# Bias vectors in 23 shifted copies instead of 128, and tables read from them in longer runs

## The chip, the cores and the metric

The kernel runs on one core of a Trainium2 chip. The metric is the device time of one launch in microseconds (us): the median of a few runs. One further execution was taken with the hardware profiler, and all rows below come from it. The engines are TensorE (PE, matmuls; PEld is its weight load), VectorE (DVE), ScalarE (ACT), GpSimd (POOL) and SyncE (SP, which issues the DMAs here).

## What is computed

The reference is two networks, one after the other, over 256 tokens of width 1024: a block of feed-forward, retention and differential attention in two layers, and a second block in two layers, of feed-forward, a mixer, and feed-forward. The mixer of the second block's first layer is a short convolution, that of its second layer a dilated attention with three groups. Only that attention uses the data that the change touches: a learned bias by distance, the same along each diagonal of a score matrix.

```python
def band_bias(rel_bias_g, dilation, n_steps):
    i = jnp.arange(BLOCK)[:, None]
    j = jnp.arange(2 * BLOCK)[None, :]
    step = BLOCK + i - j
    in_band = (step >= 0) & (step <= n_steps)
    bucket = t5_bucket(jnp.clip(step, 0, n_steps) * dilation)
    bias = rel_bias_g[bucket]
    return jnp.transpose(bias, (2, 0, 1)).astype(jnp.float32), in_band
...
    logits = jnp.einsum('bsnqhd,bsnkhd->bsnhqk', qs, kb) + bias
```

All matmuls of weights are done in three parts (high by high, high by low, low by high) to keep single precision.

## The kernel before

**Weights.** All weights pass once, in order, through a stream of units. A unit is a tile of 128 partitions by up to 2048 numbers (1 MB). `issue_dma` (line 113) has SP load it into `raw`, of which there are four buffers; `pre_act` (L127) makes the high part `whi` on ACT, in two halves, and `pre_dve` (L136) the low part `wlo` on DVE. When the second half's low part is written, the unit's `raw` buffer is free and SP may load the unit four places on. `whi` and `wlo` have three buffers. SP works through its DMAs strictly in the order of the program, and all of them go out on one queue.

**Feed-forward.** `ffn` takes 22 units of gate and up weights (`gu...`), each of them 48 matmuls of 128x256 at L161, and then 16 units of the down product (`dn...`), whose eight results are added into `h` at L291. Near its start, `norm_end` (L249) reads the sum of squares of the layer before.

**Bias vectors.** `bias_vectors` is called just ahead of the second block's first-layer second feed-forward. For each of five tables `v` it makes a vector of 256 numbers for each of 16 heads: a matmul with a one-hot matrix (L801) and a copy to `bt` (L802), a tile on 16 partitions, one for each head. Then five DMAs (L804), put into the program by `later` four slots apart, write `bt` to the DRAM tensor `ztab`: each vector 128 times, one copy for each partition of the later tables.

**Tables.** The attention of the last layer works on four heads at a time, from nine weight units (three groups of queries, keys and values; L920). `load_table` (L818) reads a head's table from `ztab` to a tile `tab` of 128 partitions by 5 by 128 numbers. A row pitch of 255 within copies of 256 shifts each partition by one number against the last, which gives the diagonals. `scores` adds the table to the products of queries and keys in one DVE instruction (L858), which also gives the row's extreme value; ACT takes the exponential. For queries and keys, ACT squares the product into `qsq` (L933), and DVE sums it (L935). `out1` writes `aon` on DVE (L886), which PE then transposes.

Which instruction of an engine comes where is settled when the program is built, by a scheduler that works with estimated durations; every engine then runs its own list in order.

Of the kernel before, what the change touches and what calls it, by code (L numbers as in the profile page):

```python
# [29 lines left out]
NG = 144  # L30

C_ID, C_RC, C_RS, C_DC, C_DS, C_MASK, C_DEC = 0, 128, 400, 672, 944, 1216, 1488
NC1 = 1488 + 4 * 272
# [5 lines left out]
def build(ctx, tc, ins, out, upto=None):  # L39
# [3 lines left out]

    # ------------------------------------------------------------------ pools
    keep = ctx.enter_context(tc.tile_pool(name="keep", bufs=1))
# [34 lines left out]
    qk_g = keep.tile([128, 6], F32, name="qk_g")  # L80
    ztab = dram.tile([16, 5, 128, 256], F32, name="ztab")

    # --------------------------------------------------------- weight stream
    units = []
# [32 lines left out]
    def pre_act(most=2):  # L117
        """High parts of the next half units, as far as the slots reach."""
        while most and st["half"] // 2 < min(st["done"] + NSPLIT, NU):
            i, b = divmod(st["half"], 2)  # L120
            n = units[i][1] // 2
            if b == 0:
                his[i] = (wp.tile([128, 2048], F32R, tag="whi", name="whi"),
                          wp.tile([128, 2048], F32R, tag="wlo", name="wlo"))
            hi, lo = his[i]
            c = slice(b * n, b * n + n)
            ACT.activation(hi[:, c], raws[i][:, c], AF.Copy)  # L127
            pend.append((i, b, c))
            st["half"] += 1
            most -= 1  # L130

    def pre_dve():
        """Low parts of what pre_act has done."""
        for i, b, c in pend:
            hi, lo = his[i]
            DVE.tensor_tensor(out=lo[:, c], in0=raws[i][:, c], in1=hi[:, c], op=ALU.subtract)  # L136
            if b == 1:
                raws.pop(i)
                issue_dma(i + 1 + NRAW)
        pend.clear()  # L140
# [15 lines left out]

    # ------------------------------------------------------- small utilities
    def mm3(ps, wh, wl, xh, xl, start, stop, late=False):
# [37 lines left out]

    # ------------------------------------------------------------------ norms
    # The gain goes into the split operand; the factor of a token goes into
    # the results of the products that use it.
    nst = {}  # L200
# [37 lines left out]
    def norm_end():  # L238
        T = nst["T"]
        ms = bank("o")  # L240
        PE.matmul(ms[:, 0:T], ones, nst["ssq"][:, 0:T], start=True, stop=True)
        if nst["fin"] is not None:
            ms2 = bank("t")
            PE.matmul(ms2[:, 0:T], ones, nst["ssq2"][:, 0:T], start=True, stop=True)
        x = nrm.tile([128, T1], F32, tag="nx", name="nx", bufs=1)
        t = nrm.tile([128, T1], F32, tag="nt", name="nt", bufs=1)
        r = nrm.tile([128, T1], F32, tag="r", name="r")
        xv, tv, rv = x[:, 0:T], t[:, 0:T], r[:, 0:T]
        DVE.tensor_scalar(out=xv, in0=ms[:, 0:T], scalar1=EPS, scalar2=None, op0=ALU.add)  # L249
        fin = nst["fin"]  # L250
        if fin is None:
            rsqrt_wide(xv, rv, tv)
            return r
        # Both norms in one factor: 1 / ((ms + eps) (ms2 / (ms + eps) + eps)).
        x2 = nrm.tile([128, T1], F32, tag="nx2", name="nx2", bufs=1)
        DVE.scalar_tensor_tensor(out=x2[:, 0:T], in0=xv, scalar=EPS, in1=ms2[:, 0:T], op0=ALU.mult, op1=ALU.add)
        rsqrt_wide(x2[:, 0:T], rv, tv)

        def residual():
            r1 = nrm.tile([128, T1], F32, tag="r", name="r1")  # L260
            t1 = nrm.tile([128, T1], F32, tag="nx2", name="t1", bufs=1)
            rsqrt_wide(xv, r1[:, 0:T], t1[:, 0:T])
            for d in range(KD):
                hv = h[:, d, T1 - T:T1]
                DVE.scalar_tensor_tensor(out=hv, in0=hv, scalar=fin[:, d:d + 1], in1=r1[:, 0:T],
                                         op0=ALU.mult, op1=ALU.mult)
        later(8, residual)
        return r
# [15 lines left out]

    # ------------------------------------------------------- products into h
    def add_to_h(d, ps, scale, T, perm=False):
# [6 lines left out]
    def out_product(yhi, ylo, order, off, T, first, nxt, perm=False, ready=None):  # L293
        """[1024 x 1024] product into h; its first `first` outputs wait with
        their last two K tiles for what is still under way."""
        tiles = {}
# [112 lines left out]

    # ------------------------------------------- retention + diff attention  # L410
    swap_pair = [i ^ 1 for i in range(32)]
    swap_half = [(i ^ 8) if i < 16 else i for i in range(32)]

    def mix_first(l, cst, nxt):
# [27 lines left out]

        # values: to token-major
        d_cols = ((0, 16), (16, 144), (144, 272))
# [14 lines left out]

        # differential attention of one head  # L460
        dsmall = {}
# [91 lines left out]

        # the first 16 queries of all differential heads
        def small_scores():
# [65 lines left out]

        # retention of one head: token tiles (0, 128), (128, 256), (256, 272)
        def ret_scores(hd):
# [115 lines left out]

    # -------------------------------------------------------------- conv mixer  # L740
    def mix_conv(nxt):
# [48 lines left out]

    # ------------------------------------------------------- dilated attention
    def bias_vectors(sb):
        hot = sb.tile([33, 5, 256], F32, name="hot")
        rb = sb.tile([33, 48], F32, name="rb")
        bt = sb.tile([16, 5, 256], F32, name="bt")
        SP.dma_start(hot, ins["onehot"].rearrange("b (v x) -> b v x", v=5))
        POOL.memset(rb[32:33, :], NEG)
        SP.dma_start(rb[0:32, :], ins["rel_bias"])
        for v, g in enumerate((0, 1, 2, 0, 0)):
            p = bank("t", 16, (256,))  # L800
            PE.matmul(p, rb[:, g * 16:(g + 1) * 16], hot[:, v, :], start=True, stop=True)  # L801
            ACT.activation(bt[:, v, :], p, AF.Copy)  # L802
        for v in range(5):
            later(4 * v, lambda v=v: SP.dma_start(ztab[:, v, :, :], bt[:, v:v + 1, :].to_broadcast([16, 128, 256])))  # L804

    def mix_attn(nxt):
# [7 lines left out]
        def load_table(hd):  # L814
            t = tmp.tile([128, 5, 128], F32, tag="tab", name="tab", bufs=4)
            z = ztab[hd]
            src = bass.AP(tensor=z.tensor, offset=z.offset + 127, ap=[[255, 128], [128 * 256, 5], [1, 128]])
            SP.dma_start(t, src)  # L818
            tabs[hd] = t.rearrange("p v x -> p (v x)")

        def turn(qd, g, w, ps, f):
            """Normalised queries or keys of four heads to feature-major."""
            qn = tmp.tile([128, 8, 64], F32, tag="qn", name="qn")
# [14 lines left out]
        def scores(qd, pr, a):  # L838
            """Two heads, in the two row halves of the array."""
            if flight["n"] >= 2:  # L840
# [3 lines left out]
            s = [bank("b") for i in range(2)]  # L844
            # column, group, first key, keys
            blocks = (((0, 1, 0, 128), (128, 2, 0, 128), (256, 0, 0, 256)) if a == 0 else
# [6 lines left out]
            for i in range(2):  # L853
                hq = pr * 2 + i
                tab = tabs[qd["i"] * 4 + hq][:, 128 - 128 * a:640 - 128 * a]
                e = tmp.tile([128, 512], F32, tag="e", name="e", bufs=3)
                nm = tmp.tile([128, 1], F32, tag="anm", name="anm", bufs=3)
                DVE.tensor_tensor_reduce(out=e, in0=s[i], in1=tab, scale=-1.0, scalar=3e38, op0=ALU.add, op1=ALU.min,  # L858
                                         accum_out=nm)
# [23 lines left out]
        def out1(qd):  # L883
            DVE.reciprocal(qd["sum"], qd["sum"])
            on = tmp.tile([128, 8, 64], F32, tag="aon", name="aon")
            DVE.tensor_tensor(out=on, in0=qd["o"].rearrange("p a h d -> p (a h) d"),  # L886
# [16 lines left out]
        for qi in range(4):  # L903
# [5 lines left out]
            for g in range(3):  # L909
                for w in range(3):  # L910
# [19 lines left out]
                    else:  # L930
                        sq = tmp.tile([128, 8, 64], F32, tag="qsq", name="qsq")
                        ss, x, y, t = (tmp.tile([128, 2, 4], F32, tag="q" + n, name="q" + n, bufs=3) for n in "sxyt")
# [23 lines left out]

    # ---------------------------------------------------------------- program
    def gcol(c):
# [109 lines left out]

# [1 line left out]
def _tiles(w):  # L1070
    """[K, M] -> [M / 128, 128, K / 128, 128]: for each 128 columns, the rows by partition."""
    K, M = w.shape
# [119 lines left out]
```

## Time and profile before

| | us |
|---|---|
| median of 3 runs | 2331.13 (2330.07 to 2332.43) |
| span of the profiled execution | 2330.6 |
| PE busy | 2249.6 (97%) |
| DVE busy | 1567.0 (67%) |
| ACT busy | 1063.3 (46%) |
| POOL busy | 165.6 (7%) |

The profiled execution's time is its span, 2330.6 us, so it lies within the three runs. The profile gives for each engine the busy time, the busy share in 40 slices of the span, the clock that TensorE was granted, the bytes that the DMA engines moved, and a chain: the work that ended last, followed back from the last instruction to what released each step. A PE that is busy for 97% of the span leaves few places where another engine or a DMA can be what ends last; the slices show where these are.

### The profile page before, as it was taken

What the parts mean: (1) busy time and instruction counts of PE and PEld (TensorE: products, weight loads), DVE (VectorE), ACT (ScalarE), POOL (GpSimd) and SP (SyncE); (2) the same over time, 40 slices, a digit from 0 to 9 for tenths busy, and PEclk for the clock granted to TensorE, in tenths of its full rate; (3) what the DMA queues carried; (4) which work ended last, traced back from release to release, by engine and by line L of the source; (5) the groups of instructions that cost most, each with busy time, mean ns of one, the idle gap of its engine ahead of it and who ended that gap; (6) DMA issues with size and microseconds to landing.
All of it is one profiled execution on the core that took longest, in us unless ns stands there. A gap on an engine that the chain in (4) does not pass through costs nothing.

```text
span 2330.6 us, 43868 instructions
## 1 busy us (share of the span) xinstructions
PE 2249.6 (97%) x18324; PEld 2211.8 (95%) x18324; DVE 1567.0 (67%) x2880; ACT 1063.3 (46%) x1721; POOL 165.6 (7%) x590
## 2 busy tenths in 40 slices
PE   9999999999999999999999995499999999999999
PEld 9999989999999998999999995499999999999999
DVE  7766878766765877766975873375875555545874
ACT  5444435444444444545444441244444455555543
POOL 1000140000000021000000000000000333330000
PEclk9999999999999999999999997699999999999999
DMA  7546325445545433546545568845545644442543
GB/s 278 175 140 211 127 91 182 175 149 201 181 141 194 154 127 132 192 151 214 183 164 198 199 172 137 207 158 202 196 170 176 220 156 168 141 164 94 186 154 130
DMA packets 80514, 395.58 MB, mean 170 GB/s; under 512 B 7067, under 2 KB 28827, under 8 KB 46012
## 3 DMA queue, kind: packets, MB, share of 16 engines
q1 hardware_dynamic: 80316, 392.78, 50.5%
q8 instruction: 143, 2.34, 0.4%
q14 instruction: 55, 0.45, 0.1%
HBM read 381.22 MB, written 11.53 MB: 169 GB/s over the span
## 4 chain that ended last, share of the span: by engine, by line
PE 90%; DMA 4%; DVE 2%; POOL 1%; issue 1%; ACT 1%; SPq 0%; POOLq 0%; ACTq 0%; DVEq 0%
PE ps_mm L161 42%; PE ps_b L161 23%; PE ps_a L161 11%; PE ps_mm L920 9%; DMA raw<-in_gu2b_dram 4%; PE ps_o L877 1%; PE ps_b L851 1%; DVE wlo L136 1%; PE ps_a L866 1%; POOL rt L192 1%; PE ps_t L832 0%; PE ps_b L469 0%; ACT whi L127 0%; DMA h<-in_h_dram 0%; POOL ry L195 0%
## 5 line engine op out<-in xcount | busy, mean ns | idle before, releaser
L136 DVE TENSOR_TENSOR wlo<-raw,whi 128x1024 fp32r<-128x1024 f32 (+1 forms) x792 | 857.7, 1114 | 332.0 <-ACT whi L127 331.4
L127 ACT ACTIVATE whi<-raw 128x1024 fp32r<-128x1024 f32 (+1 forms) x792 | 730.5, 966 | 737.1 <-issue 311.5
L161 PE MATMUL ps_mm<-xhi,wlo 128*128 128x256 f32 (+1 forms) x1904 | 544.0, 286 | 0.5 <-DVE wlo L136 0.5
L161 PE MATMUL ps_mm<-xlo,whi 128*128 128x256 f32 (+1 forms) x1904 | 541.9, 285 | 0.0
L161 PE MATMUL ps_mm<-xhi,whi 128*128 128x256 f32 (+1 forms) x1904 | 534.8, 286 | 0.0
L161 PEld LDWEIGHTS ps_mm<-xhi,wlo 128*128 128x128 f32 x1904 | 359.5, 189 | 3.2 <-issue 2.2
L161 PEld LDWEIGHTS ps_mm<-xlo,whi 128*128 128x128 f32 x1904 | 358.9, 189 | 2.1 <-issue 1.9
L161 PEld LDWEIGHTS ps_mm<-xhi,whi 128*128 128x128 f32 x1904 | 359.2, 189 | 1.4 <-issue 1.1
L161 PE MATMUL ps_b<-xhi,wlo 128*128 128x256 f32 (+1 forms) x1032 | 296.5, 288 | 50.4 <-DVE wlo L136 49.7
L161 PE MATMUL ps_b<-xlo,whi 128*128 128x256 f32 (+1 forms) x1032 | 295.4, 286 | 0.0
L161 PE MATMUL ps_b<-xhi,whi 128*128 128x256 f32 (+1 forms) x1032 | 290.9, 287 | 0.0
L161 PEld LDWEIGHTS ps_b<-xhi,wlo 128*128 128x128 f32 x1032 | 197.0, 191 | 52.3 <-DVE wlo L136 50.3
L161 PE MATMUL ps_mm<-fh,wlo 128*128 128x256 f32 (+1 forms) x704 | 199.4, 283 | 0.0
L161 PE MATMUL ps_mm<-fh,whi 128*128 128x256 f32 (+1 forms) x704 | 199.0, 283 | 0.0
L161 PE MATMUL ps_mm<-fl,whi 128*128 128x256 f32 (+1 forms) x704 | 198.9, 283 | 0.0
L161 PEld LDWEIGHTS ps_b<-xlo,whi 128*128 128x128 f32 x1032 | 196.9, 191 | 0.6 <-issue 0.4
L161 PEld LDWEIGHTS ps_b<-xhi,whi 128*128 128x128 f32 x1032 | 197.1, 191 | 0.1
L373 ACT ACTIVATE th<-gs 128x256 f32<-128x256 f32 (+1 forms) x176 | 72.7, 420 | 262.4 <-DVE gs L372 262.4
L920 PE MATMUL ps_mm<-wlo,xhi 128*128 128x256 f32 x576 | 164.2, 286 | 1.9 <-ACT vT L929 1.9
L920 PE MATMUL ps_mm<-whi,xlo 128*128 128x256 f32 x576 | 164.2, 285 | 0.0
L920 PE MATMUL ps_mm<-whi,xhi 128*128 128x256 f32 x576 | 163.0, 283 | 0.0
L161 PE MATMUL ps_a<-xhi,wlo 128*128 128x256 f32 (+1 forms) x520 | 148.9, 286 | 12.1 <-DVE wlo L136 10.9
(353 smaller groups left out, 4322.0 us busy)
## 6 DMA issues: line engine op xcount, KB each, us to landing
raw<-in_gu_dram SPq DMA_DIRECT2D x87, 1024.0 KB, 4.8
raw<-in_dn_dram SPq DMA_DIRECT2D x64, 704.0 KB, 4.1
raw<-in_gu1b_dram SPq DMA_DIRECT2D x44, 1024.0 KB, 4.8
raw<-in_gu2b_dram SPq DMA_DIRECT2D x44, 1024.0 KB, 4.8
raw<-in_qkv_dram SPq DMA_DIRECT2D x36, 1024.0 KB, 4.8
raw<-in_win_dram SPq DMA_DIRECT2D x28, 1024.0 KB, 4.8
raw<-in_dn1b_dram SPq DMA_DIRECT2D x32, 704.0 KB, 4.1
raw<-in_dn2b_dram SPq DMA_DIRECT2D x32, 704.0 KB, 4.0
```

Source lines behind the costliest of these rows:

```text
L127: ACT.activation(hi[:, c], raws[i][:, c], AF.Copy)
L136: DVE.tensor_tensor(out=lo[:, c], in0=raws[i][:, c], in1=hi[:, c], op=ALU.subtract)
L161: PE.matmul(ps, a, b, start=start and i == 0, stop=stop and i == 2)
L192: POOL.tensor_tensor(out=t, in0=y, in1=y, op=ALU.mult)
L373: ACT.activation(th[:, 0:T], gs[:, 0:T], AF.Tanh, scale=0.5)
L851: PE.matmul(s[i][:, c:c + n], q[p, pr, g, a * 128:a * 128 + 128], k[p, pr, g, k0:k0 + n], start=True, stop=True)
L866: PE.transpose(tp[:, b, :], e[:, b * 128:(b + 1) * 128], ident)
L877: PE.matmul(qd["o"][:, a, hq, :], pT[:, b, :], qd["v"][:, kt, g, hq * 64:hq * 64 + 64], start=b == 0, stop=b == 3)
L920: PE.matmul(ps[:, a, :], x, y, start=k == 0 and n == 0, stop=k == KD - 1 and n == 2)
```

## The change

The bias vectors of a head are kept together, as one run of 5 x 256 = 1280 numbers, and this run is stored 23 times for each head, by four DMAs of 6, 6, 6 and 5 copies. Each of them now needs all of `bt`. Partition p = 8a + b of a table takes copy a + b, from the place 127 - p on, so that 16 + 8 - 1 = 23 copies are enough. `load_table` reads 1152 numbers in one run for each partition, where there were five runs of 128. Of these 1152 each of the two score blocks uses four pieces of 128, 256 apart, so the DVE instruction of `scores` now has operands of 4 by 128. `tab` grows from 640 to 1152 numbers a partition, in four buffers; `qsq` and `aon` go from two buffers to one. The diff also removes comments, which shifts line numbers.

```diff
+NCOPY = 15 + 7 + 1
...
-    ztab = dram.tile([16, 5, 128, 256], F32, name="ztab")
+    ztab = dram.tile([16, NCOPY, 1280], F32, name="ztab")
...
-        for v in range(5):
-            later(4 * v, lambda v=v: SP.dma_start(ztab[:, v, :, :], bt[:, v:v + 1, :].to_broadcast([16, 128, 256])))
+        for c in range(0, NCOPY, 6):
+            n = min(6, NCOPY - c)
+            later(2 * c, lambda c=c, n=n: SP.dma_start(
+                ztab[:, c:c + n, :], bt.rearrange("h v x -> h (v x)").unsqueeze(1).to_broadcast([16, n, 1280])))
...
-            t = tmp.tile([128, 5, 128], F32, tag="tab", name="tab", bufs=4)
+            t = tmp.tile([128, 1152], F32, tag="tab", name="tab", bufs=4)
             z = ztab[hd]
-            src = bass.AP(tensor=z.tensor, offset=z.offset + 127, ap=[[255, 128], [128 * 256, 5], [1, 128]])
+            src = bass.AP(tensor=z.tensor, offset=z.offset + 127, ap=[[1280 - 8, 16], [1280 - 1, 8], [1, 1152]])
             SP.dma_start(t, src)
-            tabs[hd] = t.rearrange("p v x -> p (v x)")
+            tabs[hd] = (t[:, 128:1152].rearrange("p (v x) -> p v x", v=4)[:, :, 128:256],
+                        t[:, 0:1024].rearrange("p (v x) -> p v x", v=4)[:, :, 0:128])
...
-                tab = tabs[qd["i"] * 4 + hq][:, 128 - 128 * a:640 - 128 * a]
+                tab = tabs[qd["i"] * 4 + hq][a]
...
-                DVE.tensor_tensor_reduce(out=e, in0=s[i], in1=tab, scale=-1.0, scalar=3e38, op0=ALU.add, op1=ALU.min,
+                ev, sv = (z.rearrange("p (v x) -> p v x", v=4) for z in (e, s[i]))
+                DVE.tensor_tensor_reduce(out=ev, in0=sv, in1=tab, scale=-1.0, scalar=3e38, op0=ALU.add, op1=ALU.min,
                                          accum_out=nm)
...
-            on = tmp.tile([128, 8, 64], F32, tag="aon", name="aon")
+            on = tmp.tile([128, 8, 64], F32, tag="aon", name="aon", bufs=1)
...
-                        sq = tmp.tile([128, 8, 64], F32, tag="qsq", name="qsq")
+                        sq = tmp.tile([128, 8, 64], F32, tag="qsq", name="qsq", bufs=1)
```

The program's order changes in two places, and by a few rows on each engine. On SP, in the feed-forward that follows `bias_vectors`, the list before reads as follows (`hot` and `rb` are the one-hot matrix and the biases, `raw<-in_gu2b_dram` is a weight unit):

```order
L796 DMA hot<-in_onehot_dram 33x1280
L798 DMA rb<-in_rel_bias_dram 32x48
L113 DMA raw<-in_gu2b_dram 128x2048
L804 DMA ztab<-bt 16x128x256 x2
L113 DMA raw<-in_gu2b_dram 128x2048
L804 DMA ztab<-bt 16x128x256
L113 DMA raw<-in_gu2b_dram 128x2048
L804 DMA ztab<-bt 16x128x256 x2
L113 DMA raw<-in_gu2b_dram 128x2048 x13
```

And after the change:

```order
L798 DMA hot<-in_onehot_dram 33x1280
L800 DMA rb<-in_rel_bias_dram 32x48
L115 DMA raw<-in_gu2b_dram 128x2048 x3
L807 DMA ztab<-bt 16x6x1280 x3
L807 DMA ztab<-bt 16x5x1280
L115 DMA raw<-in_gu2b_dram 128x2048 x13
```

Two weight units that stood behind two and three stores now stand ahead of all of them, and the four stores follow one another.

On ACT, at the first queries and keys of the attention (`qsq` the squares, `whi` high parts of weights, `vT` the values), before:

```order
L127 ACTIVATE whi<-raw 128x1024
L933 ACTIVATE qsq<-ps_mm 128x512
L127 ACTIVATE whi<-raw 128x1024 x2
L933 ACTIVATE qsq<-ps_mm 128x512
L127 ACTIVATE whi<-raw 128x1024 x2
L929 ACTIVATE vT<-ps_mm,rc 128x256 x2
```

And after the change:

```order
L129 ACTIVATE whi<-raw 128x1024
L939 ACTIVATE qsq<-ps_mm 128x512
L129 ACTIVATE whi<-raw 128x1024 x3
L939 ACTIVATE qsq<-ps_mm 128x512
L129 ACTIVATE whi<-raw 128x1024
L935 ACTIVATE vT<-ps_mm,rc 128x256 x2
```

One high part moved from behind the second square to ahead of it.

## Rows read from the trace of the kernel before

**Rows 1.** The page: span, and busy tenths of PE in 40 slices.

```profile
span 2330.6 us, 43868 instructions
...
PE   9999999999999999999999995499999999999999
```

**Rows 2.** Chain of work, 1350 to 1560 us: start us, us, what (xcount).

```profile
1386.37 0.53 PE ps_t L801 x2
...
1391.04 59.40 DMA raw<-in_gu2b_dram x2
...
1454.12 37.74 DMA raw<-in_gu2b_dram
...
1494.31 5.49 PE ps_b L161 x24
...
1505.87 2.84 PE ps_mm L161 x24
```

**Rows 3.** Stretches of two feed-forwards: length, then PE, PEld, DVE, ACT, POOL busy; PEclk.

```profile
1384.88:1633.41 248.53, 189.75 (x1534) 186.70 (x1533) 129.86 (x215) 87.27 (x136) 0.00 (x0) 0.88 0.69 174
1640.77:1821.22 180.45, 180.45 (x1527) 180.28 (x1526) 130.25 (x215) 85.94 (x132) 0.00 (x0) 1.00 0.53 182
```

**Rows 4.** PE by line, 1384.88 to 1633.41: busy, mean ns | idle before, releaser.

```profile
L161 PE MATMUL ps_b<-xhi,wlo 128*128 128x256 f32 x113 | 33.9, 300 | 47.9 <-DVE wlo L136 47.2 <-issue 0.7
...
L161 PE MATMUL ps_a<-xhi,wlo 128*128 128x256 f32 x52 | 15.6, 300 | 10.9 <-DVE wlo L136 10.9
...
L801 PE MATMUL ps_t<-hot,rb 33*16 33x256 f32 x8 | 2.4, 382 | 0.0
```

**Rows 5.** DMA issues of the whole span: xcount, KB each, median us to landing.

```profile
raw<-in_gu2b_dram SPq DMA_DIRECT2D x44, 1024.0 KB, 4.8
...
ztab<-bt SPq DMA_DIRECT2D x5, 2048.0 KB, 38.3
...
tab<-ztab SPq DMA_DIRECT2D x16, 320.0 KB, 5.2
```

**Rows 6.** DMA, 1395 to 1400 us, where only `ztab` stores run.

```profile
DMA packets 503, 0.52 MB, mean 103 GB/s; under 512 B 0, under 2 KB 503, under 8 KB 503
```

**Rows 7.** DMA, 2328.4 to 2328.9 us: the last store of `h` from 128 partitions.

```profile
DMA packets 142, 0.13 MB, mean 262 GB/s; under 512 B 14, under 2 KB 142, under 8 KB 142
```

**Rows 8.** SP in order of time, 1376 to 1500 us: start us, us.

```profile
1383.60 7.34 SPq L804 DMA_DIRECT2D ztab<-bt  x2
1391.04 19.42 SPq L113 DMA_DIRECT2D raw<-in_gu2b_dram  x1
```

**Rows 9.** ACT in order of time, 1380 to 1500 us [idle before <-releaser].

```profile
1398.95 0.35 ACT L802 ACTIVATE bt<-ps_t 16x256 f32<-16x256 f32 x1
...
1429.88 2.00 ACT L127 ACTIVATE whi<-raw 128x1024 fp32r<-128x1024 f32 x2 [21.51 <-DMA raw<-in_gu2b_dram]
```

**Rows 10.** PE alone, 1421 to 1422 us: length, busy (xcount), PEclk, DMA share, GB/s.

```profile
1421.00:1422.00 1.00, 0.34 (x3) 1.00 0.82 101
```

**Rows 11.** DMA, 1824.9 to 1830.4 us, while the first four tables land.

```profile
DMA packets 2695, 1.77 MB, mean 322 GB/s; under 512 B 80, under 2 KB 2640, under 8 KB 2640
```

**Rows 12.** Stretches of the attention: columns as Rows 3, then DMA share, GB/s.

```profile
1821.00:1870.00 49.00, 47.13 (x387) 46.93 (x386) 27.49 (x42) 23.08 (x31) 21.68 (x70) 0.97 0.59 200
1870.00:1920.00 50.00, 50.00 (x431) 48.30 (x430) 27.56 (x50) 26.25 (x41) 21.39 (x70) 1.00 0.46 161
```

**Rows 13.** ACT in order of time, 1808 to 1850 us [idle before <-releaser].

```profile
1831.29 1.06 ACT L127 ACTIVATE whi<-raw 128x1024 fp32r<-128x1024 f32 x1 [7.28 <-issue]
...
1835.21 0.58 ACT L933 ACTIVATE qsq<-ps_mm 128x512 f32<-128x512 f32 x1
```

**Rows 14.** DVE in order of time, 1808 to 1850 us.

```profile
1833.57 0.67 DVE L935 TENSOR_REDUCE qs<-qsq 128x8 f32<-128x512 f32 x1
```

**Rows 15.** DVE by line, 1790 to 2180 us: busy us, mean ns | idle before.

```profile
L858 DVE CUSTOM_DVE_ANT_0 e<-ps_b,tab 128x512 f32<-128x512 f32 x32 | 21.3, 686 | 16.0 <-PE ps_b L851 9.2 <-ACT e L860 2.5 <-PE ps_a L866 2.4
L824 DVE TENSOR_TENSOR qn<-ps_mm,qy 128x512 f32<-128x512 f32 x24 | 16.5, 688 | 14.3 <-POOL qy L941 14.3
```

## The prediction

> **What bounds the kernel now.** I read the slices first. PE is busy for nine tenths or more in 38 of 40 slices and for 5 and 4 tenths in slices 25 and 26, from about 1398 to 1515 us [rows 1]. So PE bounds the kernel everywhere but in one hole of two slices, and an edit pays only if it reaches that hole, or costs only if it opens another. The chain of waits names what fills the hole: two stretches in which the chain is a weight unit's DMA, 59.40 and 37.74 us long [rows 2], where such a load takes 4.8 us as a rule [rows 5]. The lines of PE in that stretch say the same from the other end: PE sat idle 47.9 + 10.9 = 58.8 us for `wlo`, and nothing else [rows 4]; ACT had waited for the load ahead of that [rows 9].
>
> Why is the load late? The DMAs of one queue go through in order. Between the unit that came in time and the first late one stand two `ztab` stores [rows 8], of 2 MB each, which take 38.3 us to land [rows 5]. While they alone run, the queue moves 103 GB/s [rows 6]. The five of them are 5 x 16 x 128 x 1024 B = 10.49 MB, at that rate 101.8 us, of which PE's stock of weights covered the first 38 (from 1383.60 us [rows 8] to 1421.3 us, where PE ran dry [rows 10]).
>
> [...] From `norm_end` to the last result, this feed-forward took 248.53 us; the next one, with the same products, took 180.45 us with PE busy all the time [rows 3]. The difference is 68.1 us. It has 58.8 us of idle time in it, four of the five bias products (8 matmul rows for them in the stage [rows 4], 0.53 us a product [rows 2], 2.1 us), and 7.2 us that remain for the slow clock.
>
> **The change part by part.** *The stores.* New size: 16 x 23 x 5120 B = 1.884 MB instead of 10.49 MB. The trace has no store in runs of 5120 B. Its cost lies between two readings of [rows 6]: if packets set the pace (503 in 5 us, 101 a us), 368 of them take 3.7 us; if bytes do, 1.884 MB at 103 GB/s take 18.3 us. The last store of `h` goes out in packets of the same 1 KB at 262 GB/s, from 128 partitions [rows 7], so the packet is not what holds `ztab` back; its source on 16 partitions is left, and that stays. I take 18.3 us, the bytes.
>
> [...]
>
> Do 18.3 us hide? Each new store needs all of `bt`, whose last copy ends at 1398.95 + 0.35 = 1399.3 us [rows 9]; and two more weight units now stand ahead of the stores in SP's list. PE ran dry at 1421.3 us for want of the unit that was issued at 1391.04 us [rows 8]. From a landing to the first matmul the last late unit took 1494.31 - (1454.12 + 37.74) = 2.45 us [rows 2]. So that unit had to land by 1418.9 us. A unit keeps PE for 48 matmuls, 2 x 2.84 = 5.7 us [rows 2]; the next must land by 1424.5 and the third by 1430.2 us. The first two are ahead of the stores now; the third is the first behind them and lands at 1399.3 + 18.3 + 4.8 = 1422.4 us [rows 5]. It has 7.8 us to spare, so I cost the stores at nothing. What hides them is the stock of three prepared and four loaded units. If the stores took over 18.3 + 7.8 = 26.1 us (under 72 GB/s), each further us would be one of PE. The five bias products, 2.65 us on PE, stay.
>
> So the stage should take 180.45 + 2.1 = 182.6 us, and the gain is 248.53 - 182.6 = **65.9 us**.
>
> *The table loads.* Bytes grow from 16 x 320 KB to 16 x 576 KB, packets shrink from 640 to 128 a table. The first four tables landed amid 322 GB/s [rows 11]. Four tables of 1.31 MB take 4.1 us at that rate, four of 2.36 MB take 7.3 us: 3.3 us more, if bytes set it; below nothing if the 512 B packets did, by a few us. The nearest place where this is seen is the attention's start, where ACT waited 7.28 us for the weights that follow the first four tables [rows 13]; PE lost 1.9 us in that stretch [rows 12]. I take nothing, since from 1870 us on the DMA engines are busy for 0.46 of the time and PE doesn't wait [rows 12], and keep 0 to 3.3 us for the first four tables.
>
> *The DVE instruction with 4 x 128 operands.* 32 of them at 0.686 us; the trace has no such form of this operation. A neighbour whose operands are 8 x 64, one of them repeated, takes 0.688 us for as many numbers [rows 15]. I take no change. Were it to double, 22 us would come onto a DVE that is busy for 27.6 of 50 us there [rows 12]; only at the attention's end, where four steps follow one another, could PE see it, 4 x 0.7 = 2.8 us.
>
> *The single buffers.* The second `qsq` may not be written until DVE has summed the first. The sum ends at 1833.57 + 0.67 = 1834.24 us, the next square began at 1835.21 us [rows 13, 14], and one high part of 1.06 us [rows 13] now stands ahead of it. The cover is about 2 us. Behind a late square on ACT would wait the high parts, and PE behind these. `aon` is used once for four heads and is read just after it is written. Both cost nothing.
>
> **Sum.** 2330.6 - 65.9 = 2264.7 us for the span. The median before lies 0.5 us over the profiled span, so 2265.2 us.
>
> **Rivals.** (A) *Some of the hole stays.* If the new stores ran at half the rate, 36.6 us, the third unit would land 10.5 us late, and the slow clock behind it would cost up to 3 us (5.49 for 2.84 [rows 2]): 2279 us. Against it stands the steady rate of [rows 6], which is from the same partitions. (B) *The attention pays.* The 3.3 us of the first four tables, 2.8 us at the end, and a wait of 1 us or two at `qsq` give 2265 + 4 to 8, 2269 to 2273 us. For it speaks that PE already loses time at that place [rows 12]; against it that the next 50 us, with DMA, DVE and ACT busy for about half, lose nothing. (C) *The other side: the table loads run on one DMA engine.* The new source is written as 16 x 8 x 1152, the tile as 128 x 1152; if they were not spread, one engine at a sixteenth of 322 GB/s, 20 GB/s [rows 11], needs 29 us a table, 117 us for four heads, and 29 us for its sixteenth of their nine weight units: 146 us. Four heads take PE some 75 us (9 x 5.7 us of weights, and the attention itself). 71 us too many, four times, give 2265 + 284 = 2549 us. It is slower than before only from one engine on: two would need 88 us, 13 too many, and 2317 us. Against it: the old source of 128 x 5 x 128 did spread (322 GB/s [rows 11]), and the tile's side is unchanged.
>
> [...]
>
> (D) *The change doesn't reach the hole:* the loads were late for something else, and PE waits as before: 2331 us. Only [rows 5, 6, 8] would have to mislead together.
>
> **How the numbers follow.** Forecast, 2262.5 to 2268: 0.78; the lower end is the 2.1 us of bias products, should they hide. B: 0.12. A: 0.06. C: 0.02 for slower, D: 0.02. A measurement of this kernel can tell about 0.2%, 4.7 us, from no change; all but C and D are far beyond that: faster 0.96, same 0.02, slower 0.02. The range takes in the forecast and B, and the nearer part of A: 2262 to 2275 us.
>
> **What would show it.** Right: no slice with PE under nine tenths near 1400 us, this feed-forward at about 182.6 us, the four stores landed by 1418 us at 103 GB/s, PE never waiting for `wlo` there, its clock at 1.00. The attention should take as long as before, its DVE instruction 0.69 us, and the tables land within some 8 us. Wrong: stores over 26 us, a PE wait at the attention's first values, or a table that lands after 20 us.

## The result, and the profile after

| | before | after |
|---|---|---|
| median, us | 2331.78 (2330.07 to 2332.57, 4 runs) | 2266.49 (2265.12 to 2267.78, 4 runs) |
| span of the profiled execution, us | 2330.6 | 2264.4 |
| second block's first-layer second feed-forward, us | 248.53 | 182.94 |
| PE busy | 97% | 99% |

The ratio is 0.9722, with an interval of 0.971 to 0.9734: 65 us less.

The page of after, where [rows 1] stood before: the span, PE's busy tenths and granted clock in 40 slices, and the traffic of the chip's DRAM (HBM); behind it the HBM line of before's page.

```profile
span 2264.4 us, 43866 instructions
...
PE   9999999999999999999999999999999999999999
...
PEclk9999999999999999999999999999999999999999
...
HBM read 385.41 MB, written 2.93 MB: 172 GB/s over the span
```

```profile
HBM read 381.22 MB, written 11.53 MB: 169 GB/s over the span
```

The two slices with 5 and 4 tenths are gone and no other has opened. 8.60 MB less is written, and the stores lost 10.49 - 1.88 = 8.61 MB.

The two feed-forwards of [rows 3], in after: length, then PE, PEld, DVE, ACT and POOL busy, the granted clock, DMA share and GB/s.

```profile
1385.84:1568.78 182.94, 182.94 (x1534) 180.70 (x1533) 130.25 (x215) 86.89 (x136) 0.00 (x0) 1.00 0.59 189
1576.14:1756.61 180.47, 180.47 (x1527) 180.30 (x1526) 130.28 (x215) 85.96 (x132) 0.00 (x0) 1.00 0.53 182
```

PE is busy for all of the first one, at a granted clock of 1.00. It is 248.53 - 182.94 = 65.6 us shorter; the span is 66.2 us shorter. The remaining 0.6 us comes from two other stages and is told of at the end.

SP of after in order of time, 1376 to 1500 us, for [rows 8]: start us, us.

```profile
1381.09 13.87 SPq L115 DMA_DIRECT2D raw<-in_gu2b_dram  x3
...
1400.29 9.26 SPq L807 DMA_DIRECT2D ztab<-bt  x4
1409.65 61.04 SPq L115 DMA_DIRECT2D raw<-in_gu2b_dram  x13
```

The DMA engines of after, 1402 to 1419 us, while the stores run, for [rows 6]:

```profile
DMA packets 386, 1.73 MB, mean 102 GB/s; under 512 B 48, under 2 KB 48, under 8 KB 386
```

By the trace's packet records the store's 368 packets of 5120 B pass from 1401.1 to 1419.7 us, 18.6 us, at the rate that packets of 1 KB had before. The unit behind them is late for ACT, but not for PE. ACT of after in order of time, 1380 to 1450 us, for [rows 9]; the bracket is the idle time before and its releaser:

```profile
1399.91 0.35 ACT L804 ACTIVATE bt<-ps_t 16x256 f32<-16x256 f32 x1
...
1423.89 2.01 ACT L129 ACTIVATE whi<-raw 128x1024 fp32r<-128x1024 f32 x2 [3.54 <-DMA raw<-in_gu2b_dram]
```

Where ACT waited 21.51 us before, it waits 3.54 us now, and PE still has prepared weights.

In the attention, the table loads in after, by tile; and the rate while the first four land, 1760.28 to 1771.53 us, which answers to [rows 11].

```profile
L822 SPq DMA_DIRECT2D tab<-ztab x16: 526/557/655, 1756.7 to 2006.3; - x16
...
DMA to landing us min/median/max: 5.3/7.3/13.9
```

```profile
DMA packets 645, 2.81 MB, mean 250 GB/s; under 512 B 79, under 2 KB 79, under 8 KB 590
```

The loads became slower: 7.3 us each for 5.2, and 250 GB/s for 322 (both rates have weight packets in them). ACT's wait at the attention's start, for [rows 13], and the DVE instruction, for [rows 15]:

```profile
1766.68 1.06 ACT L129 ACTIVATE whi<-raw 128x1024 fp32r<-128x1024 f32 x1 [7.28 <-issue]
```

```profile
L864 DVE CUSTOM_DVE_ANT_1 e<-ps_b,tab 128x512 f32<-128x512 f32 x32 | 21.3, 687 | 16.0 <-PE ps_b L856 9.2 <-PE ps_a L872 3.3 <-issue 1.9
```

Both are as they were: 7.28 us, and 687 ns for 686.

### The profile page after: what moved, and what is told of

Read it like the earlier page. It is cut to its first block, busy times and chain, and to the rows that moved or that the text cites. A ratio compares the mean times of both kernels' runs of the same rounds, so it can differ in the third digit from the quotient of the medians.

```text
span 2264.4 us, 43866 instructions
## 1 busy us (share of the span) xinstructions
PE 2243.0 (99%) x18324; PEld 2206.0 (97%) x18324; DVE 1567.6 (69%) x2880; ACT 1063.2 (47%) x1721; POOL 166.9 (7%) x590
## 4 chain that ended last, share of the span: by engine, by line
PE 95%; DVE 2%; POOL 1%; issue 1%; ACT 1%; DMA 0%; SPq 0%; POOLq 0%; DVEq 0%
PE ps_mm L163 44%; PE ps_b L163 24%; PE ps_a L163 12%; PE ps_mm L926 9%; PE ps_o L883 1%; PE ps_b L856 1%; PE ps_a L872 1%; DVE wlo L138 1%; POOL rt L194 1%; PE ps_t L837 0%; PE ps_b L471 0%; ACT whi L129 0%; DMA h<-in_h_dram 0%; POOL ry L197 0%; POOL rt L196 0%
```

## The experiments

The theory: `ztab` held the weight loads up in SP's queue, for its bytes divided by the 103 GB/s that its source on 16 partitions allows; the smaller number of bytes is the whole gain. The rivals: the longer runs, or the new order on SP, carry a part of it; and, for the other edits, that they cost something.

**Fewer copies alone.** The kernel before, with its tables of 256 numbers, its 1 KB packets and its order on SP, but 23 copies (its tables are read from other places, so the biases aren't the reference's):

```diff
-    ztab = dram.tile([16, 5, 128, 256], F32, name="ztab")
+    ztab = dram.tile([16, 5, 24, 256], F32, name="ztab")
...
-            later(4 * v, lambda v=v: SP.dma_start(ztab[:, v, :, :], bt[:, v:v + 1, :].to_broadcast([16, 128, 256])))
+            later(4 * v, lambda v=v: SP.dma_start(ztab[:, v, 0:23, :], bt[:, v:v + 1, :].to_broadcast([16, 23, 256])))
...
-            src = bass.AP(tensor=z.tensor, offset=z.offset + 127, ap=[[255, 128], [128 * 256, 5], [1, 128]])
+            src = bass.AP(tensor=z.tensor, offset=z.offset + 127, ap=[[43, 128], [24 * 256, 5], [1, 128]])
```

> The kernel before with one thing changed: each of the five vectors is stored 23 times instead of 128, still in runs of 1 KB by five stores, and the tables are still read in five runs of 512 B (from shifted places that fit into 23 copies, so the biases are not those of the reference). The bytes stored are those of the changed kernel, 1.884 MB. If the gain is the bytes of a store from 16 partitions (my theory: 103 GB/s, and what the stock of weights covers is free), the feed-forward after the bias vectors takes 182 to 184 us, PE waits nowhere in it, and the time is 2266 to 2269 us. If the longer runs of stores or tables, or the new order of SP's list, carry a part of the gain, that part is missing here: 2275 us or more, up to 2331.

Measured: 2266.12 us (2265.26 to 2267.45), ratio 0.9725 (0.9709 to 0.9741). The feed-forward, as in [rows 3]:

```profile
1384.93:1567.87 182.94, 182.94 (x1534) 180.70 (x1533) 130.57 (x215) 87.16 (x136) 0.00 (x0) 1.00 0.58 189
```

That is the whole gain, to the hundredth of a us in this stage, without longer runs, without the new order and without the new form on DVE.

**All but fewer copies.** The changed kernel, with its runs and its order, but 128 copies again, in four stores of 32:

```diff
-NCOPY = 15 + 7 + 1
+NCOPY = 128
...
-        for c in range(0, NCOPY, 6):
-            n = min(6, NCOPY - c)
-            later(2 * c, lambda c=c, n=n: SP.dma_start(
+        for c in range(0, NCOPY, 32):
+            n = min(32, NCOPY - c)
+            later(c // 4, lambda c=c, n=n: SP.dma_start(
```

> The changed kernel with 128 copies in place of 23, in runs of 5 KB, by four stores of 32 copies. Longer runs and the new order stay, the bytes are those of before, 10.49 MB. Theory (bytes): 101.8 us of stores from about 1400 us on, the first unit behind them lands at about 1507 us and was needed at 1431, so PE loses 76 us and some 3 us by the clock: 2340 to 2350 us, slower than the kernel before. Rival (packets): 2048 packets at the old 101 a us are 20 us, hidden: 2266 to 2268 us.

Measured: 2347.05 us (2345.67 to 2348.42), ratio 1.007 (1.005 to 1.009). PE's waits for `wlo` from 1380 to 1640 us (total, times, longest) in before and in this run, then SP's stores, the stage, and the DMA engines from 1410 to 1500 us in this run:

```profile
PE ps_b L161 <- DVE wlo L136: 47.2, 2, 34.0
PE ps_a L161 <- DVE wlo L136: 10.9, 1, 10.9
```

```profile
PE ps_b L163 <- DVE wlo L138: 77.1, 1, 77.1
```

```profile
1401.35 19.84 SPq L807 DMA_DIRECT2D ztab<-bt  x4
```

```profile
1386.90:1649.78 262.88, 185.82 (x1534) 183.38 (x1533) 131.01 (x215) 87.46 (x136) 0.00 (x0) 0.85 0.72 164
```

```profile
DMA packets 1852, 9.26 MB, mean 103 GB/s; under 512 B 48, under 2 KB 48, under 8 KB 1850
```

The hole is back, and larger. The bytes are those of before and so is the rate, 103 GB/s with packets five times as long. But the stage takes 262.88 us where it took 248.53, and PE waits once for 77.1 us where it waited three times, 58.1 us in all. The stores now stand behind the last copy to `bt`: the first is issued 14.45 us after the stage's start (1386.90), where it was issued 1.28 us ahead of it before, 15.7 us later. By the packet records the last of them is through 117.9 us after the stage's start, for 103.2 before: 14.7 us later, and the stage is 14.35 us longer. The weight unit behind all stores is the same one in both orders, so the later start is enough to account for this; no run has the later start alone. So the new form has a price of its own, 14 us at 128 copies, which with 23 copies lies under what the stock of weights covers.

**The same bytes from 128 partitions.** The kernel before with all its copies. The source of the stores is spread, each head's vector lying on eight partitions; for this the weights of the bias product are repeated on DVE, and `ztab` has its first two dimensions exchanged, which the excerpt leaves out:

```diff
-        bt = sb.tile([16, 5, 256], F32, name="bt")
+        bt = sb.tile([128, 5, 256], F32, name="bt")
+        rx = sb.tile([33, 48, 8], F32, name="rx")
...
+        DVE.tensor_copy(rx, rb.unsqueeze(2).to_broadcast([33, 48, 8]))
...
-            PE.matmul(p, rb[:, g * 16:(g + 1) * 16], hot[:, v, :], start=True, stop=True)
+            PE.matmul(p, rx[:, g * 16:(g + 1) * 16, :].rearrange("b h r -> b (h r)"), hot[:, v, :], start=True, stop=True)
...
-            later(4 * v, lambda v=v: SP.dma_start(ztab[:, v, :, :], bt[:, v:v + 1, :].to_broadcast([16, 128, 256])))
+            later(4 * v, lambda v=v: SP.dma_start(
+                ztab[v].rearrange("h (r c) x -> (h r) c x", r=8), bt[:, v:v + 1, :].to_broadcast([128, 16, 256])))
```

> The kernel before with 128 copies in runs of 1 KB, all 10.49 MB of them, but stored from 128 partitions: the weights of the bias product are repeated eight times (one small DVE copy more), so that 8 partitions hold each head's vector and each stores 16 copies. If what paces the store is its source on 16 partitions: 262 GB/s or more, at most 40 us for all five, with weight units between them, 2266 to 2275 us. If it is the bytes written to DRAM, whatever their source: 103 GB/s as before, and 2320 to 2335 us.

Measured: 2268.10 us (2266.86 to 2268.8), ratio 0.9731 (0.9716 to 0.9746). Its DMA issues (count, KB each, median us to landing), the rate from 1405 to 1407.8 us, where only stores run, and the stage:

```profile
ztab<-bt SPq DMA_DIRECT2D x5, 2048.0 KB, 14.2
```

```profile
DMA packets 1059, 1.08 MB, mean 387 GB/s; under 512 B 0, under 2 KB 1059, under 8 KB 1059
```

```profile
1385.28:1569.81 184.53, 184.13 (x1534) 181.74 (x1535) 130.03 (x216) 87.58 (x137) 0.00 (x0) 1.00 0.66 234
```

10.49 MB in 1 KB packets, still with weight units between the stores (behind the first and the third; before, behind the second and the third), and all but 1.6 us of the gain: 387 GB/s instead of 103. Of the 1.6 us, 0.4 are a pause of PE and the rest is longer busy time (184.13 for 182.94), whose cause is open. With the two runs before this one, the cause is settled: bytes over the rate of 16 partitions. Either factor alone closes the hole.

In these runs the rate went with the partitions of the source: 102 to 103 GB/s from 16 of them, with packets of 1 KB and of 5 KB, and 387 GB/s from 128. Why 16 partitions have this rate no run shows.

**Twice the copies.** Where does the cover end? The changed kernel with 46 copies, which makes the stores as long as rival A had them:

```diff
-NCOPY = 15 + 7 + 1
+NCOPY = 46
...
-        for c in range(0, NCOPY, 6):
-            n = min(6, NCOPY - c)
-            later(2 * c, lambda c=c, n=n: SP.dma_start(
+        for c in range(0, NCOPY, 12):
+            n = min(12, NCOPY - c)
+            later(c, lambda c=c, n=n: SP.dma_start(
```

> The changed kernel with 46 copies in place of 23 (four stores of 12, 12, 12 and 10 copies, of which the tables read the first 23): the store's cost doubled. Theory: 36.6 us in place of 18.3, the first unit behind the stores lands about 18.5 us later than in the changed kernel, where some 7 to 8 us were to spare; PE loses 10 to 12 us and up to 3 us more by the clock: 2277 to 2282 us. If the stock of weights covers twice as much as I worked out: 2266 to 2268 us. If it covered nothing more than the 18.3 us: 2285 to 2289 us.

Measured: 2281.63 us (2280.97 to 2282.93), ratio 0.979 (0.9776 to 0.9805). PE's waits, the stage, and the chain of waits from 1430 to 1460 us:

```profile
PE ps_b L163 <- DVE wlo L138: 11.1, 1, 11.1
PE ps_mm L163 <- issue: 0.9, 1, 0.9
```

```profile
1386.18:1584.09 197.91, 185.99 (x1534) 183.34 (x1533) 129.50 (x216) 86.56 (x136) 0.00 (x0) 0.97 0.64 184
```

```profile
1410.97 31.81 DMA raw<-in_gu2b_dram
...
1445.25 5.49 PE ps_b L163 x24
```

PE ran dry at 1445.25 - 11.1 = 1434.15 us. This stage began 1.30 us later than before's, so that is 1432.85 us in before's time; the prediction had the third unit's limit at 1430.2 us for the landing and 2.45 us from there to PE, 1432.65. Without the other 0.9 us, which end at 1432.75 us and for which the profile shows no releaser, PE would have run dry that much earlier, so the cover was sized right to within 1 us. The stage grew by 15.0 us: 11.9 us of idle time (both waits) and 3.05 us of busy time (185.99 for 182.94), most of it the group behind the pause, 5.49 us for 2.84, in a stage whose mean granted clock is 0.97 where after has 1.00.

**One copy.** The changed kernel with its stores all but taken away and its tables read from unshifted rows, so that the biases aren't the reference's:

```diff
-NCOPY = 15 + 7 + 1
+NCOPY = 1
...
-            src = bass.AP(tensor=z.tensor, offset=z.offset + 127, ap=[[1280 - 8, 16], [1280 - 1, 8], [1, 1152]])
+            src = bass.AP(tensor=z.tensor, offset=z.offset, ap=[[1, 128], [1, 1152]])
```

> The changed kernel with one copy stored (82 KB in one store) and the tables read from it one number on from partition to partition (the mirrored diagonals, so not the reference's biases). This is the floor: nearly no store. If the 23 copies are hidden as I worked out: within 2 us of the changed kernel, 2264.5 to 2268 us, and ACT's wait for the first weight unit behind the stores (3.5 us in the changed kernel) is gone without PE gaining. If some of the hole stays in the changed kernel: faster by that part, 3 us or more.

Measured: 2265.69 us (2264.52 to 2267.52), ratio 0.9722 (0.9709 to 0.9735). ACT from 1403 to 1430 us, and the DMA engines while the first four tables land:

```profile
1421.76 2.01 ACT L129 ACTIVATE whi<-raw 128x1024 fp32r<-128x1024 f32 x2 [1.09 <-PE ps_mm L163]
```

```profile
DMA packets 659, 2.93 MB, mean 365 GB/s; under 512 B 78, under 2 KB 78, under 8 KB 590
```

ACT's wait of 3.54 us goes and the time stays, so the 18 us of stores are wholly hidden. The tables, though, now load at 365 GB/s for the same bytes in the same runs; the three last runs below ask why.

**Single buffers alone.** The kernel before with one buffer each for `aon` and `qsq`:

```diff
-            on = tmp.tile([128, 8, 64], F32, tag="aon", name="aon")
+            on = tmp.tile([128, 8, 64], F32, tag="aon", name="aon", bufs=1)
...
-                        sq = tmp.tile([128, 8, 64], F32, tag="qsq", name="qsq")
+                        sq = tmp.tile([128, 8, 64], F32, tag="qsq", name="qsq", bufs=1)
```

> The kernel before with only the two single buffers (qsq, aon). My step put them at nothing: 2330 to 2333 us, the hole unchanged. The attention took 1.6 us less in the profile of the changed kernel; if that comes of the order at its start, which moves with the single buffers, it should show here too, 324.1 us in place of 325.7 between the two results; if it is chance of the clock, it should not follow the order.

Measured: 2332.08 us (2327.38 to 2334.85, 10 runs), ratio 1.0002 (0.9993 to 1.0011). They cost nothing that can be measured. In its profile the attention takes 316.3 us, from the last result of the feed-forward ahead of it to its own last, as in after (316.1) and unlike before (317.7); ACT's order at its start is that of after. But fewer copies alone, with before's order, have 316.1, and 46 copies, with after's order, 317.6. So the order doesn't decide this; the last section comes back to it.

**An even start.** The changed kernel with every row of a table starting at a multiple of 512 B, with no shift:

```diff
-            src = bass.AP(tensor=z.tensor, offset=z.offset + 127, ap=[[1280 - 8, 16], [1280 - 1, 8], [1, 1152]])
+            src = bass.AP(tensor=z.tensor, offset=z.offset + 128, ap=[[1280, 16], [1280, 8], [1, 1152]])
```

> The changed kernel with table rows that start at multiples of 512 B (copy a + b at place 128 for each partition, so no shift and not the reference's biases); sizes and counts as in the changed kernel. There a table packet of 4.6 KB took longer than a weight packet of 8 KB has per byte, and the tables landed in 7.3 us in place of 5.2. If the odd start is the cause: the tables land in 4 to 5.5 us. If it is that all partitions read the same small region of DRAM: as in the changed kernel, about 7 us. The time is the same in both cases, 2264.5 to 2268 us, since the attention hides the loads.

Measured: 2266.53 us (2265.76 to 2267.3), ratio 0.9725 (0.9712 to 0.9738); a table lands in 7.3 us, as in after. The DMA engines while the first four land:

```profile
DMA packets 641, 2.79 MB, mean 251 GB/s; under 512 B 78, under 2 KB 78, under 8 KB 590
```

It isn't the odd start.

**Both cures.** The changed kernel with 24 copies, stored by one DMA from 128 partitions (`bt` spread as in the run with 128 copies from 128 partitions, which the excerpt leaves out):

```diff
-NCOPY = 15 + 7 + 1
+NCOPY = 24
...
-        for c in range(0, NCOPY, 6):
-            n = min(6, NCOPY - c)
-            later(2 * c, lambda c=c, n=n: SP.dma_start(
-                ztab[:, c:c + n, :], bt.rearrange("h v x -> h (v x)").unsqueeze(1).to_broadcast([16, n, 1280])))
+        later(0, lambda: SP.dma_start(
+            ztab.rearrange("h (r c) x -> (h r) c x", r=8),
+            bt.rearrange("h v x -> h (v x)").unsqueeze(1).to_broadcast([128, 3, 1280])))
```

> The changed kernel with the vectors on 128 partitions as in the run with the wide source: one store of 24 copies, each partition writing three runs of 5 KB. Stores at 262 GB/s or more: 5 to 8 us in place of 18.6. Both what was 103 GB/s and ACT's wait of 3.5 us go, but they were hidden: 2264.5 to 2268 us, the same as the changed kernel. If the stores still cost something there, faster by 3 us or more.

Measured: 2266.63 us (2265.36 to 2268.15), ratio 0.9725 (0.9712 to 0.9739). Its store:

```profile
ztab<-bt SPq DMA_DIRECT2D x1, 1920.0 KB, 7.3
```

It lands in 7.3 us, and the kernel takes as long: once hidden, a faster store is worth nothing.

**The form of the table's rows.** Three kernels, one edit each on the load. The first, of one copy, was to have 16 by 8 rows at the places of one copy. Its steps of 8 and 1 run together into 128 rows of step 1, so it is the run with one copy once more, with its biases.

```diff
-            src = bass.AP(tensor=z.tensor, offset=z.offset + 127, ap=[[1280 - 8, 16], [1280 - 1, 8], [1, 1152]])
+            src = bass.AP(tensor=z.tensor, offset=z.offset, ap=[[8, 16], [1, 8], [1, 1152]])
```

> The one-copy kernel again (not the reference's biases), with the same addresses in another form: the table's source is written as 16 by 8 rows, as in the changed kernel, where the one-copy run had 128 rows. There a table packet took 178 ns (median), in the changed kernel 311 ns, with an aligned start 315 ns. If what slows the packet is the 16 by 8 form (how the rows are dealt out to the DMA engines): about 300 ns again, tables landing in about 7 us. If it is the copies' places in DRAM: 178 ns and 6 us. The time is the same either way, 2264 to 2268 us.

Measured, in one run: 2265.64 us, beside 2330.97 for the kernel before; tables in 6.0 us. Inconclusive.

The second keeps the two steps apart (9 and 1, from two copies). The places in DRAM stay within a few KB, as with one copy; only the form is that of the change, and the biases aren't the reference's.

```diff
-            src = bass.AP(tensor=z.tensor, offset=z.offset + 127, ap=[[1280 - 8, 16], [1280 - 1, 8], [1, 1152]])
+            src = bass.AP(tensor=z.tensor, offset=z.offset, ap=[[9, 16], [1, 8], [1, 1152]])
```

> The run before this one could not tell: rows of 16 by 8 with steps of 8 and 1 are 128 rows with a step of 1, and the program held them as that. Here the steps are 9 and 1, from two copies a head (not the reference's biases), so the 16 by 8 form stays, and all rows still lie within 5.2 KB of DRAM. If the form slows the table packets: about 310 ns and 7 us to landing. If the places in DRAM do (rows 5 KB apart in the changed kernel): 178 ns and 6 us. The time is 2264 to 2268 us either way.

Measured, in one run: 2265.93 us, beside 2333.7 for the kernel before. The first four tables:

```profile
DMA packets 637, 2.74 MB, mean 245 GB/s; under 512 B 79, under 2 KB 79, under 8 KB 591
```

The third has the change's biases in full, as 32 by 4 rows from 40 copies, stored from 128 partitions as above:

```diff
-            src = bass.AP(tensor=z.tensor, offset=z.offset + 127, ap=[[1280 - 8, 16], [1280 - 1, 8], [1, 1152]])
+            src = bass.AP(tensor=z.tensor, offset=z.offset + 127, ap=[[1280 - 4, 32], [1280 - 1, 4], [1, 1152]])
```

> The changed kernel with the store from 128 partitions (40 copies, 3.28 MB, 8 to 10 us) and the table rows taken as 32 by 4 in place of 16 by 8 (35 copies are then read, the biases are those of the reference). If the form of 16 by 8 slows the tables: packets near 180 ns and landing in about 6 us. If the places in DRAM do: about 310 ns and 7 us as before. Both the stores and the tables are hidden, so the time is that of the changed kernel, 2264.5 to 2268 us.

Measured: 2266.90 us (2265.67 to 2267.82), ratio 0.9724 (0.9708 to 0.974); a table lands in 5.9 us. The first four:

```profile
DMA packets 675, 3.07 MB, mean 417 GB/s; under 512 B 78, under 2 KB 78, under 8 KB 589
```

Rows written as 16 by 8 load at 245 to 251 GB/s wherever they lie; as 32 by 4 at 417, as 128 at 365 GB/s. By the packet records a table packet takes 311, 314 and 316 ns (median) in the three runs with 16 by 8 rows, and 178 ns in those with 32 by 4 and with 128. So the form slows the load, not the place and not the start. None of it moves the time: the loads are hidden in all of these kernels.

## Why the prediction was right, and where it wasn't

*The cause.* Right, and now shown: fewer bytes alone give the whole gain, and so, but for 1.6 us, does the wider source alone. Longer runs and the new order gave nothing of it.

*The size.* The comparison with the next feed-forward gave 182.6 us for this one; it took 182.94. That is what made the forecast close. The idle time alone, 58.8 us, would have missed 7 us. (Of these 58.8 us, which the prediction puts to `wlo` alone, [rows 4] puts 0.7 us to "issue".) What the prediction leaves for the slow clock, 7.2 us, shows in PE's busy time: 189.75 us at the mean clock of [rows 3], 0.88, and 182.94 us at 1.00 in after, 6.8 us less. Behind before's longest pause, from 1494.31 to 1499.80 us, the granted clock was 0.50.

*The stores.* Priced by bytes at 18.3 us; they took 18.6 us. Priced by packets it would have been 3.7 us. The third unit was put at 1422.4 us; ACT was released at 1423.89, which is 1422.9 us in before's time, as this stage began 0.96 us later. The spare time was right too, to within 1 us, as 46 copies show.

*The order on SP.* Right: the prediction counted both sides of it, that the stores wait for the last copy to `bt` and that two units now stand ahead of them. It didn't say what the later start costs where the stores outlast the stock: 14 us with 128 copies. With 23 it lies under the cover. That a load waits for what stands ahead of it in the queue is seen in before's packet records: the weight unit issued at 1391.04 us moved its first packet at 1424.94 us, behind 4048 of the 4096 packets of the two stores ahead of it.

*The table loads.* This term was mis-sized. The four first tables were put at 4.1 us before and 7.3 us after by the old rate of 322 GB/s. By the packet records they took 5.3 us before (1824.93 to 1830.25) and 1771.53 - 1760.28 = 11.25 us after: 5.9 us more, outside the bound of 0 to 3.3 us. Two things were wrong. The 322 GB/s held 0.45 MB of weight packets besides the 1.31 MB of tables, and the sum left such packets out: 2.81 MB passed in after's stretch, 8.7 us at the old rate. And the rate didn't stay: the 16 by 8 form brought it down to 250 GB/s. Taking nothing for it was right, since the loads are hidden.

*ACT's wait at the attention's start.* Misread. The prediction had ACT wait 7.28 us for weights behind the first four tables. The wait is 7.28 us in before, in after and with one copy, though the tables take 5.3, 11.25 and 8.0 us, and in after it ends 4.9 us before the fourth table has landed. What it keeps step with is PE's start on the attention's products, in before and in after:

```profile
1821.19 6.95 PE ps_mm L920 x59
```

```profile
1756.58 6.95 PE ps_mm L926 x59
```

In both ACT goes on 10.10 us later (1831.29 and 1766.68). The trace's semaphore records agree: ACT waits there for the unit's load, which in after had landed by 1752.44 us, and for PE's count, which rises at 1766.61. So PE ends the wait, and no DMA; what PE gives free there isn't shown. The row itself says "issue", a wait for nothing that the profile shows; naming a DMA there went beyond the row. Rival B had most of its costs at this place. They did not come: PE's pause there is 1.87 us behind ACT's `vT`, before and after, and the attention as a whole took no longer.

*DVE and the single buffers.* Right: 687 ns, and a ratio of 1.0002.

*The other rivals.* The run with 46 copies has stores as long as in A: 15.0 us more in the stage, where A's sum gives 10.5 + 3 = 13.5. C did not occur: no table of after took longer than 13.9 us, where C has 29 us a table. While after's first four tables landed, the packets of the queue took 101.8% of 16 engines' time, weight packets among them; with rows written as 32 by 4 they took 101.2%. So by this share the engines were full with either form, and what differs is the time of a table packet, 311 and 178 ns.

*The sum.* 2265.2 us was 1.3 us low, and this is the smallest step. The span itself was put at 2264.7 us and is 2264.4. But the sum set a median of times against a span, 0.5 us apart, and in the runs here an execution's time lay 1.7 to 2.2 us above its own span, mostly near 1.8 us: 2266.16 us for the profiled 2264.4 in after, and in one later run of the kernel before 2333.7 for 2331.9. So the text ahead of the prediction is wrong to take the profiled execution's time for 2330.6; by this offset it was near 2332.4, among the slowest of the runs shown.

## What to carry to other kernels

When PE starves for weights, look at what stands ahead of them in the same queue, and price that by its bytes over a rate seen in the trace (18.3 us here, and 18.6 measured). The store of repeated data from 16 partitions was dear twice, by its 10.49 MB and by its rate, 103 GB/s where 128 partitions had 387: spread the source over 128 partitions, or store fewer copies; either was enough here. Take the worth of closing a hole from a sister stage without one, since the slow clock behind a pause (0.50 here, with 24 matmuls in 5.49 us for 2.84) doesn't show as idle time.

## What the runs showed of the hardware

**The form of the source's rows set the table loads' rate.** The same 576 KB, in the same runs of 4608 B to the same 128 partitions, land in 7.2 to 7.4 us (medians of six runs) from 16 by 8 rows and in 5.9 to 6.1 us (three runs) from 32 by 4 or 128. Why the form matters the records don't show.

**After the same short pause the clock falls or stays.** At the attention's start PE pauses for 1.87 or 1.88 us behind ACT's `vT`, in all thirteen traces. The 5 us with the pause and the 5 us after it, in before (PE busy and count first, the clock third from the end):

```profile
1838.20:1843.20 5.00, 3.13 (x21) 2.93 (x21) 3.27 (x6) 2.73 (x4) 4.51 (x13) 0.87 0.88 313
1843.20:1848.20 5.00, 5.00 (x37) 5.00 (x36) 1.39 (x2) 0.21 (x1) 3.27 (x17) 0.79 0.60 215
```

And in after:

```profile
1773.60:1778.60 5.00, 3.13 (x26) 2.93 (x25) 2.36 (x6) 2.73 (x4) 4.27 (x18) 1.00 0.93 387
1778.60:1783.60 5.00, 5.00 (x45) 5.00 (x44) 2.48 (x4) 1.96 (x3) 3.07 (x10) 1.00 0.46 157
```

In before the granted clock falls from the upper level for part of this stretch, and PE gets through 21 and 37 matmuls where after gets through 26 and 45: 13 fewer, 1.5 us at the 0.118 us that one takes at the full clock. The thirteen traces fall into two groups. Where the clock stays, in eight, the attention takes 315.8 to 316.4 us; where it falls, in five, 317.5 to 317.8 us. The change doesn't decide it: with 23 copies in before's order the clock stayed, and with 46 copies in after's order it fell. What does decide it is open; each kernel has one trace.

Before has 317.67 us and after 316.10: 1.6 us less. An earlier stage, which the change doesn't touch, took 1.0 us longer in after (135.76 us for 134.76, from the first feed-forward's last result to the next product's first); there PE's clock from 344 to 348 us is 0.57 in after and 1.00 in before. The two together, 1.6 - 1.0, make the 0.6 us by which the span's gain differs from the stage's.
